# One more seven-product output pair for the sample, T sums made behind the merges, and new planner costs, in a hybrid encoder layer

## The chip, the core and the metric

The kernel runs on one core of a Trainium2 chip. The metric is the device time of one execution, in microseconds (us); the median of the runs shown is used. The engines are PE (TensorE: matmuls and transposes), DVE (VectorE), ACT (ScalarE), POOL (GpSimd) and SP (SyncE, which here issues every DMA). They run at the same time and wait for one another on semaphores.

## What is computed

One encoder layer is applied to two batches with the same weights: a prompt of 512 tokens and a sample of 1024 tokens, each token a row of 1024 numbers. Everything is float32.

```
h = rmsnorm(x)
proj = h @ w_in            # qa ka va za | qb kb vb zb | ga gb
oa = neighbourhood_attention(qa, ka, va, rpb_a) * silu(za)
oa = oa @ w_o_a
ob = window_gqa_attention(qb, kb, vb, t5_table, sink_b) * silu(zb)
ob = ob @ w_o_b
merged = sigmoid(ga) * oa + sigmoid(gb) * ob
y = x + merged @ w_out
```

`w_in` has 5376 columns, of which `ga` and `gb` are 1024 each; `w_out` is 1024 x 1024.

## The kernel before

**Products.** Each float32 operand is split in a rounded part and a remainder (`hi` and `lo`; `whi`, `wlo` for weights, `hh`, `hl` for activations). A product is hi·hi + hi·lo + lo·hi, three matmuls for each block of 128 rows. In the dense stages (`product`, L1284 to L1286) one product of a weight chunk with half of the rows takes 4 blocks x 3 matmuls of 128 x 512, summed in one bank of PSUM. ACT makes the rounded part and DVE or POOL the remainder (`split`, L1167 and L1172).

**Order of the stages.** Norm and attention of the prompt; dense stages of the prompt, with the norm of the sample beside them; attention of the sample; dense stages of the sample. A dense phase has pairs of z chunks (SiLU gates), pairs of gate chunks, eight merges and four output pairs. Some gate pairs are computed during attention already (`fill_gates`): for the sample the last two of eight.

**Plain and seven-product pairs.** A pair is two output chunks times two halves of the tokens. `pair_classic` makes it with eight products. `pair_strassen` makes it with seven, at the price of sums: four of weight tiles (`S`), and four of activations, `T`, which all pairs of a stage share. Its products 0, 1 and 6 read `hh` and `hl`, its products 2 to 5 read `T` 1, 2, 0 and 3. `CLASSIC_S` says how many pairs of z, gates and output are plain for the sample: 1, 0 and 2 before.

**T for the output stage.** `sums` builds each of the four `T` from merged activations, in four quarters k (`m` = k and k + 4), with ten additions a quarter of 128 x 512 (`tt`, L1161), into three `S` buffers. A quarter is then split into `T`. There are eight `T` buffers (four pairs of hi and lo). The gates' `T` hold them first, then the merges' operands `uv` (loaded back from DRAM: `ot<-u_d`, two buffers), then the output's `T`, in that turn. So each stage waits for the last reader of the stage ahead.

**The planner.** The order of all instructions is worked out when the program is built, by a list scheduler (`Flow.run`): an operation has engines that may take it, an estimated duration for each, and a priority (lower is sooner); when an engine is free in the planner's own clock, it takes the first ready operation by priority. A DMA costs SP 470 ns and lands after bytes / 360 ns behind the DMAs ahead. Buffers of the tags in `IN_TURN` are given out in program order. An operation that DVE or POOL may take counts as a port operation: the planner lets no port operation begin on one of the two while the other has one. On the chip each engine executes its list strictly in that order.

**The start.** The prompt's first tile is normed in four pieces: PE spreads the norm's gains over the partitions (L1629), DVE scales a piece (L520), PE transposes it (L532), ACT and DVE split it (L537, L542). Attention weights are loaded and split beside it (L600, L602, L607), the first remainder on POOL. Projections are L761.

Of the kernel before, what the change touches and what calls it, by code (L numbers as in the profile page):

```python
# [10 lines left out]
F32 = mybir.dt.float32  # L11
# [18 lines left out]
SIDE = {5: 0, 8: 1, 11: 2, 15: 3}  # L30
CLASSIC_S = (1, 0, 2)
LEFT_PAD = 56
WAKE = 0
SOON = 10
# [106 lines left out]
class Flow:  # L141
# [10 lines left out]

    IN_TURN = {"whi", "wlo", "w32", "T", "S", "raw", "U", "C", "ot"}

# [7 lines left out]
    def op(self, choice, emit, prio, new=(), use=(), into=(), after=(), hold=(), lag=0, port=None):  # L162

        o = Op()
        choice = tuple((e, ns * self.slack if e in ("act", "dve", "pool") else ns) for e, ns in choice)
        o.choice, o.emit, o.prio, o.new, o.lag = choice, emit, prio + self.base, list(new), lag
        o.key, o.outs, o.eng = len(self.ops), [], None
        o.port = {"dve", "pool"} <= {e for e, _ in choice} if port is None else port  # L170
        o.vals = {id(v): v for v in (*new, *use, *into, *hold)}.values()
        before = {id(a): a for v in use for a in v.writers}
        before.update({id(a): a for a in after if a is not None})
        for v in into:
            for a in v.writers[:1]:
# [12 lines left out]
    def dma(self, emit, nbytes, prio, **kw):  # L188
        return self.op((("sp", 470),), lambda e: emit(), prio, lag=nbytes / 360, **kw)

# [16 lines left out]
    def run(self):  # L207
# [59 lines left out]
        while done < len(self.ops):  # L267
            for e in ready:
                while free_at[e] <= now:
                    skipped, got = [], None  # L270
                    while ready[e]:
                        item = heapq.heappop(ready[e])
                        o = item[2]
                        if o.eng is not None:
                            continue
                        ns = dict(o.choice)[e]
                        if all(room(v, n) for v, n in o.new) and not any(locked(v, e) or v.held and not v.t for v in o.vals) and not barred(o, e) and all(
# [77 lines left out]
def encoder_kernel(  # L355
# [238 lines left out]
    def att_weights(src, n, prio, engs=("pool", "dve"), place=None, after=()):  # L594
# [11 lines left out]
        def emit(e):  # L606
            engines[e].tensor_tensor(lo.t[:, :n], sv(), hi.t[:, :n].bitcast(F32), op=ALU.subtract)  # L607

        f.op(
            tuple((e, {"pool": POOL_, "dve": DVE_}[e](n)) for e in engs), emit, prio, new=[lo], use=[hi], hold=[st], after=[a],  # L610
        )
# [36 lines left out]
    def attention_phase(geo, hh, hl, h_ops, mask_d, early, late):  # L648
# [24 lines left out]
        def tables(br, g, prio):  # L673
            nb_t = tile_([P, max(2 * at[-1], 4 * GW)], F32, "bias", 2)
            first = [nb_t]
            for i in range(2 if br == "A" else 4):
# [25 lines left out]
                else:  # L702
# [15 lines left out]

                    f.op((("act", ACT_(GW)),), emit, prio, new=first, use=[raw], into=[nb_t])
                    first = []  # L720
# [7 lines left out]
        def project(br, w, t, prio):  # L728
# [10 lines left out]
            else:  # L739
# [6 lines left out]
                for q in range(2):  # L746
                    for m, v in enumerate((hh, hl)):
                        done[m, q] = f.op(
                            (("act", 960), ("dve", DVE_(512))),
                            lambda e, m=m, v=v, q=q: copy(  # L750
# [96 lines left out]
        def make_qk(br, gi, t, qk, prio):  # L847
# [23 lines left out]
            elif whole:  # L871
# [13 lines left out]
            b = f.op(  # L885
                (("dve", DVE_(P) + 165),),
                lambda _: dve.scalar_tensor_tensor(
# [4 lines left out]
            for s in slots:  # L892
# [6 lines left out]
            f.op(  # L899
                (("dve", DVE_(n) + 165),),  # L900
                lambda _: dve.scalar_tensor_tensor(
# [234 lines left out]
    def dense_phase(geo, hh, hl, h_ops, o_stores, exps_done, start, opened, tp, up, p0, p1, p2, x_t, y_t, classic, fill, after_gates=None, side=None):  # L1136
# [8 lines left out]
        any_tt = lambda n: (("dve", DVE_(n)), ("pool", POOL_(n)))  # L1145
        u_d = dpool.tile([8, P, nt], F32, tag=f"u_d{nt}", name=f"u_d{nt}")
        g_d = dpool.tile([2, 8, P, nt], F32, tag=f"g_d{nt}", name=f"g_d{nt}")
        stores = {}
# [35 lines left out]

        def sums(prio, done):

            tv = [tuple(f.value(tp, [P, 4, sn], F32R, "T", 8) for _ in range(2)) for _ in range(4)]
            ops = {}
            for k in range(4):
                blk = lambda a, kk, n: (lambda: a.t[:, kk, n * sn : (n + 1) * sn].bitcast(F32))  # L1190
                h = {(i, n, a): blk((hh, hl)[a], k + 4 * i, n) for i in range(2) for n in range(2) for a in range(2)}
# [127 lines left out]

        def pair_strassen(srcs, post, prio, mov_h, mov_t, seed=None, last=False):  # L1320
            raw = {(m, i): load_raw(srcs[m][i], prio - 2) for m, i in ((0, 0), (1, 0), (1, 1), (0, 1))}
# [33 lines left out]
            )  # L1355
            result(0, 0, p1, mul(1, mov_h(1, 0)))
            add(u2, p1, mul(2, mov_t(1)))
# [158 lines left out]
        for i in range(8):  # L1516
# [9 lines left out]
            else:  # L1526
                pair_strassen(srcs, post, 4 + i, mov_h, mov_t)
            if side:
# [243 lines left out]
```

## Time and profile before

| What | us |
|---|---|
| Median of three runs | 1145.87 (1144.78 to 1147.69) |
| Profiled execution, device time | 1146.52 |
| Its span, first to last instruction | 1144.7 |
| PE busy | 1133.8 |
| DVE busy | 854.4 |
| ACT busy | 644.9 |
| POOL busy | 308.3 |
| Sample: gates end and merges begin | about 975 |
| Sample: merges end and output pairs begin | about 1060 |

Rows of a timeline give the start in us from the span's start, the duration, the engine, the line, the operation and its tiles (out<-in). A bracket at the end gives the idle time ahead of the operation and what ended it. Rows of waits give the total, the number and the longest. A row of groups by window gives the busy time of PE, PEld (weight loads), DVE, ACT and POOL with the number of instructions, then the granted clock, the DMA engines' share and GB/s.

### The profile page before, as it was taken

What the parts mean: (1) busy time and instruction counts of PE and PEld (TensorE: products, weight loads), DVE (VectorE), ACT (ScalarE), POOL (GpSimd) and SP (SyncE); (2) the same over time, 40 slices, a digit from 0 to 9 for tenths busy, and PEclk for the clock granted to TensorE, in tenths of its full rate; (3) what the DMA queues carried; (4) which work ended last, traced back from release to release, by engine and by line L of the source; (5) the groups of instructions that cost most, each with busy time, mean ns of one, the idle gap of its engine ahead of it and who ended that gap; (6) DMA issues with size and microseconds to landing.
All of it is one profiled execution on the core that took longest, in us unless ns stands there. A gap on an engine that the chain in (4) does not pass through costs nothing.

```text
span 1144.7 us, 18482 instructions
## 1 busy us (share of the span) xinstructions
PE 1133.8 (99%) x6139; PEld 985.8 (86%) x6139; DVE 854.4 (75%) x1975; ACT 644.9 (56%) x1467; POOL 308.3 (27%) x413
## 2 busy tenths in 40 slices
PE   8999999999999999999999999999999999999998
PEld 6999988888888899999999888888888888788887
DVE  5888798497765468887778888865878755497984
ACT  5777987544433346665678988865534434343320
POOL 3653433000010054343333445330222210132110
PEclk9999999999999999999999999999999999999999
DMA  7854543488786422121221213226657335573072
GB/s 253 273 158 141 181 113 102 115 264 266 232 277 199 165 72 67 25 70 32 71 61 50 56 37 93 56 66 214 218 148 211 129 111 159 200 238 121 29 223 90
DMA packets 124705, 159.86 MB, mean 140 GB/s; under 512 B 28297, under 2 KB 66961, under 8 KB 124610
## 3 DMA queue, kind: packets, MB, share of 16 engines
q1 hardware_dynamic: 124610, 158.69, 45.4%
q8 instruction: 48, 0.79, 0.3%
q14 instruction: 47, 0.39, 0.1%
HBM read 121.93 MB, written 41.44 MB: 143 GB/s over the span
## 4 chain that ended last, share of the span: by engine, by line
PE 94%; DVE 2%; DMA 2%; ACT 1%; POOL 1%; issue 0%; SPq 0%; ACTq 0%; POOLq 0%
PE p L761 25%; PE x L1285 9%; PE x L1286 9%; PE x L1284 9%; PE x L1063 5%; PE x L1026 5%; PE x L934 4%; PE p L1284 4%; PE p L1285 4%; PE d L1284 4%; PE p L1286 4%; PE d L1286 4%; PE d L1285 4%; PE x L861 2%; DMA ot<-u_d 1%; DMA w<-in_w_att_dram 1%
## 5 line engine op out<-in xcount | busy, mean ns | idle before, releaser
L761 PE MATMUL p<-whi,hh 128*128 128x384 f32 x384 | 133.4, 348 | 0.0
L761 PE MATMUL p<-wlo,hh 128*128 128x384 f32 x384 | 133.1, 347 | 0.0
L761 PE MATMUL p<-whi,hl 128*128 128x384 f32 x384 | 132.4, 345 | 0.0
L978 ACT ACTIVATE sb<-sb,mx 128x384 f32<-128x384 f32 (+1 forms) x192 | 107.5, 563 | 22.4 <-DVE mx L969 22.2
L1167 ACT ACTIVATE whi<-raw 128x512 fp32r<-128x512 f32 (+1 forms) x140 | 81.1, 590 | 52.6 <-PE x L1285 26.2
L761 PE MATMUL p<-whi,hb 128*128 128x384 f32 x384 | 107.5, 347 | 0.0
L1172 POOL TENSOR_TENSOR wlo<-raw,whi 128x512 fp32r<-128x512 f32 (+1 forms) x29 | 40.9, 1413 | 242.4 <-ACT whi L1167 130.4
L1284 PE MATMUL x<-hh,whi 128*128 128x512 f32 x264 | 102.7, 389 | 0.0
L1285 PE MATMUL x<-hl,whi 128*128 128x512 f32 x264 | 102.7, 389 | 0.0
L1286 PE MATMUL x<-hh,wlo 128*128 128x512 f32 x264 | 102.7, 389 | 0.0
L1037 DVE TENSOR_TENSOR pp<-x,pp 128x512 fp32r<-128x512 f32 (+1 forms) x136 | 82.6, 638 | 18.9 <-ACT pp L1032 17.8
L1172 DVE TENSOR_TENSOR wlo<-raw,whi 128x512 fp32r<-128x512 f32 (+1 forms) x111 | 70.1, 645 | 30.5 <-ACT whi L1167 30.2
L1285 PE MATMUL x<-T,whi 128*128 128x512 f32 x224 | 87.5, 390 | 0.3 <-DVE T L1172 0.2
L1286 PE MATMUL x<-T,wlo 128*128 128x512 f32 x224 | 87.2, 389 | 0.0
L1284 PE MATMUL x<-T,whi 128*128 128x512 f32 x224 | 87.1, 389 | 0.0
L1032 ACT ACTIVATE pp<-x 128x512 fp32r<-128x512 f32 (+1 forms) x136 | 70.9, 560 | 22.8 <-PE x L1026 21.8
L799 POOL TENSOR_TENSOR rs_r<-rs_v,mhalf 128x4 f32<-128x4 f32 (+1 forms) x72 | 81.7, 1134 | 5.7
L1063 PE MATMUL x<-pp,v 128*128 128x256 f32 (+1 forms) x368 | 77.8, 324 | 0.8 <-DVE pp L1037 0.8
L792 POOL TENSOR_SCALAR rs_v<-ss 128x4 f32<-128x4 f32 (+1 forms) x72 | 26.2, 364 | 187.3 <-DVE ss L785 184.6
L761 PEld LDWEIGHTS p<-whi,hl 128*128 128x128 f32 x384 | 73.0, 190 | 1.3 <-issue 1.0
L761 PEld LDWEIGHTS p<-wlo,hh 128*128 128x128 f32 x384 | 73.0, 190 | 1.0 <-issue 0.5
L761 PEld LDWEIGHTS p<-whi,hh 128*128 128x128 f32 x384 | 73.0, 190 | 0.9 <-issue 0.5
(351 smaller groups left out, 2985.5 us busy)
## 6 DMA issues: line engine op xcount, KB each, us to landing
raw<-in_w_g_dram SPq DMA_DIRECT2D x76, 256.0 KB
w<-in_w_att_dram SPq DMA_DIRECT2D x46, 384.0 KB
ot<-o_d SPq DMA_DIRECT2D x36, 256.0 KB
g_d<-C SPq DMA_DIRECT2D x34, 256.0 KB
raw<-in_w_z_dram SPq DMA_DIRECT2D x32, 256.0 KB
raw<-in_w_out_dram SPq DMA_DIRECT2D x32, 256.0 KB
C<-g_d SPq DMA_DIRECT2D x24, 256.0 KB
out_dram<-C SPq DMA_DIRECT2D x23, 256.0 KB
```

Source lines behind the costliest of these rows:

```text
L761: pe.matmul(ps.t[:, :GW], part[u](k), mv.t[:, c], start=k == 0 and m == 0, stop=k == KC - 1 and m == 2,)
L799: lambda e: nc.gpsimd.tensor_tensor(r.t[:, :nn], rv.t[:, :nn], mhalf[:, :nn], op=ALU.pow),
L978: act.activation(sb.t[:, :width], sb.t[:, :width], AF.Exp, bias=mx.t[:, i : i + 1], scale=-1.0, accum_out=sm.t[:, i : i + 1],)
L1026: pe.transpose(pt.t[:, u * P : (u + 1) * P], sbs[i].t[:, c * P : (c + 1) * P], ident)
L1032: lambda e, pt=pt, pp=pp, nn=nn: act.activation(pp.t[:, 0, :nn], pt.t[:, :nn], AF.Copy),
L1037: lambda e, pt=pt, pp=pp, nn=nn: dve.tensor_tensor(pp.t[:, 1, :nn], pt.t[:, :nn], pp.t[:, 0, :nn].bitcast(F32), op=ALU.subtract),
L1063: pe.matmul(out(), v.t[:, vs], mv(), start=first, stop=last)
L1167: (("act", ACT_(n)),), lambda e: act.activation(hi(), src(), AF.Copy), prio,
L1172: lambda e: engines[e].tensor_tensor(lo(), src(), hi().bitcast(F32), op=ALU.subtract), prio,
L1284: pe.matmul(out, hi.t[:, cs], mh(), start=first and k == 0, stop=False)
L1285: pe.matmul(out, hi.t[:, cs], ml(), start=False, stop=False)
L1286: pe.matmul(out, lo.t[:, cs], mh(), start=False, stop=last and k == len(ws) - 1)
```

## The change

- `CLASSIC_S` becomes (1, 0, 1): the sample's output pair 1 is a seven-product pair, so that of four output pairs one is plain.
- `sums` for the output stage gets priorities of its own, 19.2 to 19.5 for the quarters (the merges have 12 to 19, the output pairs 20 and more). The additions of the first three quarters no longer stay in `S` until a `T` is free: each of their twelve results is stored to DRAM (`to_d`), loaded into a `U` buffer at priority 20 and split into `T` from there, in the order of `T` 1, 2, 0, 3. The last quarter is split directly.
- In the sample's last seven-product gate pair (`free_t`) the second plain product comes behind the four products that read `T`.
- The planner counts DMAs with a priority below -2 at 230 bytes per ns, and matmuls before 13 us of its clock as 1.85 times as long. It counts the bias copy 76 ns longer, the `hb` copy on ACT 40 ns longer, and the scaled remainders of k and q on DVE 105 ns shorter. `hb` buffers are given out in program order, and each weight remainder of attention counts as a port operation. `SPREAD` is 0.

```
-CLASSIC_S = (1, 0, 2)
+CLASSIC_S = (1, 0, 1)
+SEED, SPREAD, SPAN, COLD = 0, 0, 1, 13000
+EARLY_RATE = 230
...
-    IN_TURN = {"whi", "wlo", "w32", "T", "S", "raw", "U", "C", "ot"}
+    IN_TURN = {"whi", "wlo", "w32", "T", "S", "raw", "U", "C", "ot", "hb"}
...
+        if self.slack != 1:
+            o.prio += SPREAD * (hash((SEED, o.key // SPAN)) % 1000 / 1000 - 0.5)
...
-        return self.op((("sp", 470),), lambda e: emit(), prio, lag=nbytes / 360, **kw)
+        return self.op((("sp", 470),), lambda e: emit(), prio, lag=nbytes / (EARLY_RATE if prio < -2 else 360), **kw)
...
-                        ns = dict(o.choice)[e]
+                        ns = dict(o.choice)[e] * (1.85 if e == "pe" and now < COLD and o.prio > -20.5 else 1)
...
-            ... new=[lo], use=[hi], hold=[st], after=[a],
+            ... new=[lo], use=[hi], hold=[st], after=[a], port=True,
...
-                    f.op((("act", ACT_(GW)),), emit, prio, new=first, use=[raw], into=[nb_t])
+                    f.op((("act", ACT_(GW) + 76),), emit, prio, new=first, use=[raw], into=[nb_t])
...
-                            (("act", 960), ("dve", DVE_(512))),
+                            (("act", 1000), ("dve", DVE_(512))),
...
-                (("dve", DVE_(P) + 165),),
+                (("dve", DVE_(P) + 60),),
...
-                (("dve", DVE_(n) + 165),),
+                (("dve", DVE_(n) + 60),),
...
+        to_d = dpool.tile([4, 4, P, sn], F32, tag=f"to_d{nt}", name=f"to_d{nt}")
...
-        def sums(prio, done):
+        def sums(split_prio, done, prios=None):
...
+                prio = prios[k] if prios else split_prio
...
                 for j in (0, 2, 1, 3):
-                    vh, vl = tv[j]
-                    ops[j, k] = split(
-                        lambda vh=vh, k=k: vh.t[:, k], lambda vl=vl, k=k: vl.t[:, k], lambda v=t[j]: v.t[:, :sn], sn, prio,
-                        (vh, k == 0), (vl, k == 0), [t[j]],
+                    if prios and k < 3:
+                        away.append((j, k, dma(
+                            lambda j=j, k=k, v=t[j]: nc.sync.dma_start(to_d[j, k], v.t[:, :sn]), 512 * sn, prio, use=[t[j]]
+                        )))
+                    else:
+                        away.append((j, k, t[j]))
+            for j, k, v in sorted(away, key=lambda a: ((1, 2, 0, 3).index(a[0]), a[1])) if prios else away:
+                vh, vl = tv[j]
+                if prios and k < 3:
+                    o, v = v, tile_("U", 4)
+                    dma(
+                        lambda j=j, k=k, v=v: nc.sync.dma_start(v.t[:, :sn], to_d[j, k]), 512 * sn, split_prio, new=[v],
+                        after=[o],
                     )
+                ops[j, k] = split(
+                    lambda vh=vh, k=k: vh.t[:, k], lambda vl=vl, k=k: vl.t[:, k], lambda v=v: v.t[:, :sn], sn, split_prio,
+                    (vh, j not in firsts), (vl, j not in firsts), [v],
+                )
+                firsts[j] = True
...
-        def pair_strassen(srcs, post, prio, mov_h, mov_t, seed=None, last=False):
+        def pair_strassen(srcs, post, prio, mov_h, mov_t, seed=None, last=False, free_t=False):
...
-            result(0, 0, p1, mul(1, mov_h(1, 0)))
+            if not free_t:
+                result(0, 0, p1, mul(1, mov_h(1, 0)))
             add(u2, p1, mul(2, mov_t(1)))
             add(u3, u2, mul(3, mov_t(2)))
             b = mul(4, mov_t(0))
             add(u4, u2, b)
             result(1, 1, u3, b)
             result(1, 0, u3, mul(5, mov_t(3)), ALU.subtract)
+            if free_t:
+                result(0, 0, p1, mul(1, mov_h(1, 0)))
...
-                pair_strassen(srcs, post, 4 + i, mov_h, mov_t)
+                pair_strassen(srcs, post, 4 + i, mov_h, mov_t, free_t=i + 1 == 8 - fill)
...
-        mov_h, mov_t = blocks(m_ops, nh), sums(20, m_ops) if o_classic < 4 else None
+        mov_h, mov_t = blocks(m_ops, nh), sums(20, m_ops, [19.2 + 0.1 * k for k in range(4)]) if o_classic < 4 else None
```

More of the change, by code (lines that the diff above doesn't have):

```diff
@@ L609, in att_weights @@
         f.op(
-            tuple((e, {"pool": POOL_, "dve": DVE_}[e](n)) for e in engs), emit, prio, new=[lo], use=[hi], hold=[st], after=[a],
+            tuple((e, {"pool": POOL_, "dve": DVE_}[e](n)) for e in engs), emit, prio, new=[lo], use=[hi], hold=[st], after=[a], port=True,
         )
@@ L1183, in moving_sums @@
             return mov
-        def sums(prio, done):
+        def sums(split_prio, done, prios=None):
             tv = [tuple(f.value(tp, [P, 4, sn], F32R, "T", 8) for _ in range(2)) for _ in range(4)]
-            ops = {}
+            ops, away, firsts = {}, [], {}
             for k in range(4):
+                prio = prios[k] if prios else split_prio
                 blk = lambda a, kk, n: (lambda: a.t[:, kk, n * sn : (n + 1) * sn].bitcast(F32))
```

## Prediction

> **What bounds the kernel now.** I read the page first: the share of each engine, then the chain that ended last.
>
> ```profile
> span 1144.7 us, 18482 instructions
> PE 1133.8 (99%) x6139; PEld 985.8 (86%) x6139; DVE 854.4 (75%) x1975; ACT 644.9 (56%) x1467; POOL 308.3 (27%) x413
> PE 94%; DVE 2%; DMA 2%; ACT 1%; POOL 1%; issue 0%; SPq 0%; ACTq 0%; POOLq 0%
> ```
>
> TensorE (PE) is busy 1133.8 of 1144.7 us and is 94% of the chain. So a change pays in two ways only: fewer matmuls, or a shorter wait of PE. The view of PE's waits has all of the second kind:
>
> ```profile
> PE x L1629 <- DMA rb<-in_norm_row_dram: 4.4, 1, 4.4
> PE x L861 <- DVE qk L816: 1.0, 2, 0.5
> PE x L532 <- DVE xt L520: 0.9, 1, 0.9
> PE x L1063 <- DVE pp L1037: 0.8, 2, 0.6
> PE x L1026 <- DVE sb L1010: 0.3, 1, 0.3
> PE x L1285 <- DVE T L1172: 0.2, 1, 0.2
> ```
>
> Columns: total us, times, longest. The first is the load that opens the kernel, and no edit makes it shorter. The rest sums to 3.2 us. The profiled execution took 1146.52 us, 1.8 more than its span and 0.65 above the median of 1145.87; the sum below is made against it, and the prediction is the median less the same gain.
>
> A busy PE is not a paced PE, since the records of neighbouring matmuls overlap. The pace is read from starts. These are the first matmul of the sample's output stage and the first that reads a T there, in PE's timeline (start, duration):
>
> ```profile
> 1059.71 0.39 PE L1284 MATMUL x<-hh,whi 128*128 128x512 f32 x1
> ...
> 1108.67 0.39 PE L1284 MATMUL x<-T,whi 128*128 128x512 f32 x1
> ```
>
> Between them lie two plain pairs and two products of the third pair. A plain pair is 8 products of 4 x 3 matmuls, 96; so 2 x 96 + 2 x 12 = 216 matmuls in 48.96 us, **226.7 ns each**, not the 389 ns that the records last.
>
> **Term 1, one output pair with seven products.** With one plain pair instead of two, pair 1 has 7 x 12 = 84 matmuls for 96. 12 x 226.7 ns = **2.7 us** of PE work gone, on the chain. Its weights cost four more additions and three more splits on VectorE (DVE) and POOL; they are counted in term 4.
>
> **Term 2, the moved plain product of the gates.** In the last seven-product gate pair the second plain product runs after the four that read T. Each T is read for the last time one product, 12 x 226.7 ns = 2.7 us, earlier, and the merges' operands are loaded into the same buffers. What PE loses there now, and what it waits for:
>
> ```profile
> 975.15 0.40 PE L1284 MATMUL x<-T,whi 128*128 128x512 f32 x1
> 975.76 0.50 PE L1285 MATMUL x<-T,whi 128*128 128x512 f32 x1 [0.22 <-DVE T L1172]
> ...
> 979.06 0.39 PE L1284 MATMUL x<-T,whi 128*128 128x512 f32 x1
> 979.57 0.50 PE L1285 MATMUL x<-T,whi 128*128 128x512 f32 x1
> ```
>
> ```profile
> 967.11 4.66 DMA ot<-u_d
> ...
> 973.18 4.96 DMA ot<-u_d
> ```
>
> Starts 0.61 and 0.51 us apart instead of 0.23: 0.38 + 0.28 = 0.7 us lost, less than the 2.7 us by which the buffers come free. The second view (the chain, in order of time) says that loads of 4.66 and 4.96 us, two in flight, paced the T. They may start earlier with the buffers, so I take **0.7 us**, with 0 as the other end if something else paces them. The moved product's result, sigmoid and store come later too, and so does p1's U buffer; the merges' first use of U is over 20 us behind, which covers it.
>
> **Term 3, the start.** DVE's remainder of the second weight with scalings 3 and 4 of the first tile behind it, then PE's gain rows and first projections (start, duration):
>
> ```profile
> 8.72 0.96 DVE L607 TENSOR_TENSOR wlo<-w,whi 128x768 fp32r<-128x768 f32 x1 [1.17 <-ACT whi L602]
> 9.60 0.86 DVE L520 SCALAR_TENSOR_TENSOR xt<-xt,nr,x 128x256 f32<-128x256 f32 x2
> ```
>
> ```profile
> 4.42 3.75 PE L1629 MATMUL x<-rb,one 1*128 1x256 f32 x8 [4.42 <-DMA rb<-in_norm_row_dram]
> ...
> 10.92 0.67 PE L761 MATMUL p<-whi,hh 128*128 128x384 f32 x1
> ...
> 12.03 0.52 PE L761 MATMUL p<-whi,hh 128*128 128x384 f32 x1
> 12.35 0.52 PE L761 MATMUL p<-wlo,hh 128*128 128x384 f32 x1
> ...
> 16.98 0.33 PE L761 MATMUL p<-whi,hh 128*128 128x384 f32 x1
> 17.15 0.33 PE L761 MATMUL p<-wlo,hh 128*128 128x384 f32 x1
> ```
>
> Before, the planner believes the second weight to be early and puts its remainder ahead of scalings 3 and 4. At 230 bytes per ns it is planned later, and POOL's remainder of the first weight (now a port operation) bars it meanwhile, so the scalings should go first. They need the gain rows, done at 4.42 + 3.75 = 8.17; an estimate of 8.5 replaces 9.60, and the first projection comes some 0.9 us sooner than 10.92. But matmuls are 0.32 us apart there (12.03 to 12.35) and 0.17 later (16.98 to 17.15), though the clock column shows full speed: 0.9 us of slow time holds 2.8 matmuls, worth 0.5 us once fast. Some of that is lost again at the qk wait (1.0 in two waits), so I take **0.4 us**; ends: 0.9 lost, if another order starves PE, and 0.9 won, if the fast pace begins sooner as well. The Trainium skill (TensorE: Matmul & The Clock Gate, Part 1) ties the fast pace to free-running activity windows of 3.4 us; by that the 0.5 before the loss would stand, and 0.9 could not be counted on.
>
> The other planner costs (scalings of k and q, hb, the bias copy, hb in turn) change no instruction, only its order. I take 0. In attention PE waits 1.0 + 0.8 + 0.3 = 2.1 us in all, which is the most a better order wins; a worse one may lose as much. SPREAD is 0 and moves nothing.
>
> **Term 4, sums behind the merges: its cover.** The sums of the first three quarters are made while merges run, stored (12 DMAs of 256 KB), loaded again (12 more) and split. PE now needs a T at 1059.71 + (96 + 24) x 0.2267 = **1086.9**, not 1108.7. What the vector engines had free (columns: window, then busy us of PE, PEld, DVE, ACT, POOL), and how long the sums last on DVE:
>
> ```profile
> 1032.00:1064.00 32.00, 32.00 (x142) 26.49 (x142) 25.72 (x37) 11.23 (x19) 8.85 (x6) 1.00 0.37 119
> 1062.00:1090.00 28.00, 28.00 (x125) 23.20 (x124) 28.00 (x47) 9.80 (x16) 1.42 (x2) 1.00 0.05 14
> ```
>
> ```profile
> 1073.13 2.49 DVE L1161 TENSOR_TENSOR S<-S,hl 128x512 f32<-128x512 f32 x4
> ...
> 1088.17 2.48 DVE L1161 TENSOR_TENSOR C<-x,C 128x512 f32<-128x512 f32 x4
> ```
>
> DVE is full to 1090 and ends the sums at 1088.17: left alone they would be late. But it is idle 6.3 of the 32 us before 1064. One operation takes (2.49 - 0.69)/3 = 0.60 us. From 1032 to 1086.9 (54.9 us) there are 28 operations of other work before 1064 (the 37 of the first window less 9 on S and T, 16.8), 40 sums (24.0), 16 remainders of T (9.6) and some 4 us of results and pair 1's weights: about 54.4, all on DVE. POOL takes some: it was busy 8.85 us in the first window. So it fits, **0 us**, with little left. The last quarter can't start before the last merge is split, which I put some 5 us behind 1059.71, at 1065, and needs 10 x 0.60 = 6 us, then its splits: done near 1082 for the last T, which is read three products after the first. The DMAs have room: their share is 0.37 and 0.05 in the two windows. Two trips of 4.96 us cost some 10 us, covered for the quarters that were ready by 1064. If the cover is gone, PE waits in pair 1; the first two rivals price it.
>
> **Sum:** 2.7 + 0.7 + 0.4 = 3.8 us; 1146.5 - 3.8 = 1142.7 for the profiled execution, **1142.1** for the median. 0.3% of the median, about what a measurement can tell from no change, is 3.4 us: the forecast lies only just beyond.
>
> **Rivals.**
> *DVE becomes the bound at pair 1 (0.25).* For it: 54.4 of 54.9 us. Pair 1's first weights are planned behind sums and T, yet PE wants them 24 matmuls earlier, at 1081.5. POOL's help has a price:
>
> ```profile
> 1001.41 4.71 POOL L1172 TENSOR_TENSOR wlo<-raw,whi 128x512 fp32r<-128x512 f32 x3
> ...
> 1003.20 1.78 DVE L1172 TENSOR_TENSOR hl<-C,hh 128x512 fp32r<-128x512 f32 x1
> ```
>
> Beside POOL a DVE operation lasted 1.78 us, not 0.69: 1.1 lost. Two such meetings, less the 0.5 that DVE has left, make PE wait 2 x 1.1 - 0.5 = 1.7 us: 1143.8. It decides from the moment when DVE's work up to 1086.9 passes 54.9 us. Against it: the planner keeps port operations apart. The Trainium skill (SBUF — State Buffer, "SBUF: two separate sides") calls the port pair of DVE and GpSimd an exclusive lock that a two-input DVE operation also meets, the loser standing for the whole instruction; the 1.78 us agree.
>
> *The DRAM trip is late, the slower side (0.08).* SP issues in order, and it stood once for 23.7 us behind one DVE result:
>
> ```profile
> SPq L1457 <- DVE C L1161: 24.1, 3, 23.7
> ```
>
> If a store stands like that until 1088 ahead of the loads, three rounds in four U buffers follow, 3 x 4.96 = 14.9 us: T at about 1103, PE 16 us late, 1158. It decides from 7.2 us on (3.8 given back, 3.4 lost), a T later than 1094. Against it: the first three quarters are ready well before, and the loads follow in the plan's own order.
>
> *The new order loses in attention or at the start (0.12).* The 2.1 us of waits there double: 1144.2.
>
> *The moved product frees nothing (0.07).* The loads, not the buffers, pace the T; the 0.7 stays: 1142.8.
>
> **How the numbers follow.** The forecast has 0.48; its own range is 1140.4 (1.7 more from start and attention) to 1143 (the start's gain and half of term 2 missing). The range 1140.4 to 1145.6 takes in all but the DRAM trip, the far tail of the DVE rival and a doubly good order. Faster by over 0.3% (below 1142.4): most of the forecast and a lucky share of the attention case, 0.47. Within 0.3%: the rest of the forecast, the other rivals, 0.44. Slower by over 0.3% (above 1149.3): the DRAM trip and a bad tail, 0.09.
>
> **What would show it.** PE with 6127 matmuls. Term 2: no start more than 0.25 us apart in the first T products of the merges. Term 3: both pairs of scalings ahead of the second remainder, first projection near 10. Term 4: PE's starts unbroken over pair 1, DVE with S work in the merges, no wait of PE for T or wlo behind them; SP without a wait over 10 us while T loads. It is wrong if PE waits over 1 us in the output stage, or if attention's waits move by more than 2 us.

## The result, and the profile after

The changed kernel takes 1159.68 us (median of 4 runs, 1158.69 to 1161.3); the kernel before took 1146.78 beside it. The ratio is **1.0114, interval 1.0085 to 1.0142**: about 13 us slower, where 3.8 us faster was forecast. The profiled execution of after took 1159.02 us.

The page of after, in the lines that answer to those of before:

```profile
span 1156.5 us, 18522 instructions
PE 1134.1 (98%) x6127; PEld 983.1 (85%) x6127; DVE 871.0 (75%) x1980; ACT 641.1 (55%) x1474; POOL 323.2 (28%) x423
PE 83%; DVE 6%; DMA 5%; ACT 2%; POOL 2%; issue 2%; SPq 1%; DVEq 0%; POOLq 0%; ACTq 0%
```

PE has the 12 matmuls fewer, yet 0.3 us more of busy time, since those at a lower clock lasted longer. The chain tells more: PE was 94% of it and is 83%. Eleven per cent have gone to engines and transfers that PE waits for. The view of PE's waits (total us, times, longest) names them:

```profile
PE p L1305 <- ACT whi L1172: 5.4, 1, 5.4
PE x L1654 <- DMA rb<-in_norm_row_dram: 4.7, 1, 4.7
PE p L765 <- DVE hb L668: 2.1, 1, 2.1
PE x L865 <- DVE qk L820: 1.6, 3, 0.7
PE p L1307 <- DVE wlo L1177: 1.5, 1, 1.5
PE x L1305 <- ACT T L1172: 1.4, 1, 1.4
```

(Lines have moved by a few: `product` is L1305 to L1307 now, projections are L765, `split` is L1172 and L1177, sums are L1166.) The second row is the load that opens the kernel, as before. All others are new or larger. The first and the fifth are in the output stage, the third and fourth in the prompt's attention, the sixth where the merges begin.

To place the loss I added up PE's starts in the trace: for each matmul the time to the next start, less the median of that time for its shape over the traces of this study (0.227 us for 128x512). The rest, the **excess**, is what PE lost, summed by stretch (us; the last stretch of after begins with its output pairs at 1064.62):

| Stretch of the span | before | after |
|---|---|---|
| 0 to 20 (start) | 4.7 | 3.1 |
| 20 to 140 (attention of the prompt) | 5.1 | 10.5 |
| 140 to 400 (the prompt's rest) | 3.5 | 3.9 |
| 400 to 960 (sample: attention, gates) | 16.3 | 15.6 |
| 960 to 1000 (gates end, merges begin) | 1.0 | 2.1 |
| 1000 to 1060 (merges) | -0.1 | -0.1 |
| 1060 to the end (output pairs) | -0.1 | 9.5 |
| all | 30.4 | 44.7 |

(Rows add up to within 0.1 by rounding.) So 14.3 us were lost and 2.7 us of matmuls saved: 11.6 of the 11.8 us by which the span grew. **Two places carry it**, attention (5.4) and output pair 1 (9.6).

PE's timeline at the first products of pair 1 that read T (start, duration, then what ended the idle time), and the window from there (PE, PEld, DVE, ACT, POOL, granted clock, DMA share, GB/s):

```profile
1091.79 0.40 PE L1307 MATMUL p<-hh,wlo 128*128 128x512 f32 x1
1097.54 0.79 PE L1305 MATMUL p<-T,whi 128*128 128x512 f32 x1 [5.35 <-ACT whi L1172]
1098.13 0.63 PE L1306 MATMUL p<-T,whi 128*128 128x512 f32 x1
1100.27 0.80 PE L1307 MATMUL p<-T,wlo 128*128 128x512 f32 x1 [1.51 <-DVE wlo L1177]
1100.86 0.63 PE L1305 MATMUL p<-T,whi 128*128 128x512 f32 x1
1101.28 0.63 PE L1306 MATMUL p<-T,whi 128*128 128x512 f32 x1
```

```profile
1097.00:1104.00 7.00, 4.95 (x12) 3.50 (x13) 6.29 (x12) 3.40 (x7) 0.57 (x1) 0.54 0.58 173
```

Three losses stand here. PE started nothing from 1091.79 to 1097.54, 5.75 us for 0.23: 5.5 lost. Two matmuls later it stood again, 1098.13 to 1100.27: 1.9 lost. And the matmuls behind are 0.42 us apart (1100.86 to 1101.28) at a granted clock of 0.54: the other 2.1 of the 9.5.

The releaser of the first wait is a weight, `whi`, not T. ACT's timeline says why it was late:

```profile
1094.62 0.63 ACT L1172 ACTIVATE T<-U 128x512 fp32r<-128x512 f32 x1 [2.87 <-DMA U<-to_d]
...
1095.85 0.63 ACT L1172 ACTIVATE T<-U 128x512 fp32r<-128x512 f32 x1
...
1096.87 0.62 ACT L1172 ACTIVATE whi<-S 128x512 fp32r<-128x512 f32 x1
```

The two sums that this weight is made of, on DVE and POOL, stand in the timeline too:

```profile
1093.19 0.69 DVE L1166 TENSOR_TENSOR S<-raw 128x512 f32<-128x512 f32 x1
1093.95 1.27 POOL L1166 TENSOR_TENSOR S<-S,raw 128x512 f32<-128x512 f32 x1 [7.78 <-DMA C<-in_xt_s_dram]
```

The chain, in order of time, says what was behind that:

```profile
1079.85 4.25 DMA out_dram<-C
...
1084.12 0.33 SPq L1468
...
1084.56 3.98 DMA U<-to_d
...
1090.87 4.96 DMA U<-to_d
...
1095.85 0.64 ACT T L1172
...
1096.51 1.29 DVE T L1177 x2
1097.81 0.60 DVE C L1166
...
1099.61 0.61 DVE wlo L1177
1100.27 0.80 PE p L1307
```

ACT works its list in order. It stood 2.87 us for a reload of a T quarter, did the splits of T that its list has first, and only then the weight that PE wanted. That order is some 1.6 us of the wait, since the weight's second sum ended only at 1095.22 (1093.95 + 1.27) and its split lasts 0.62; the rest lies with the sums, which stood behind T's remainders on DVE (`w_first` below comes back to them). On DVE the other weight's remainder stands behind two T remainders and more in the same way. The reloads come in rounds of four U buffers, each some 4 to 5 us long, and one of them stood on SP behind a load of `C` (L1468) that waited for a store of `out_dram`.

### The profile page after: what moved, and what is told of

It reads as the page before. It is cut to its first block, busy times and chain, and to the rows that moved or that the text cites. A ratio compares the mean times of both kernels' runs of the same rounds, so it can differ in the third digit from the quotient of the medians.

```text
span 1156.5 us, 18522 instructions
## 1 busy us (share of the span) xinstructions
PE 1134.1 (98%) x6127; PEld 983.1 (85%) x6127; DVE 871.0 (75%) x1980; ACT 641.1 (55%) x1474; POOL 323.2 (28%) x423
## 4 chain that ended last, share of the span: by engine, by line
PE 83%; DVE 6%; DMA 5%; ACT 2%; POOL 2%; issue 2%; SPq 1%; DVEq 0%; POOLq 0%; ACTq 0%
PE p L765 21%; PE x L1306 8%; PE x L1307 8%; PE x L1305 8%; PE x L1067 5%; PE x L1030 4%; PE x L938 4%; PE p L1307 4%; PE p L1305 4%; PE p L1306 4%; PE d L1305 4%; PE d L1307 3%; PE d L1306 3%; PE x L865 1%; DVE S L1166 1%
## 5 line engine op out<-in xcount | busy, mean ns | idle before, releaser
L765 PE MATMUL p<-whi,hh 128*128 128x384 f32 x384 | 132.9, 347 | 0.0
L765 PE MATMUL p<-whi,hl 128*128 128x384 f32 x384 | 132.3, 345 | 0.0
L765 PE MATMUL p<-wlo,hh 128*128 128x384 f32 x384 | 131.1, 342 | 0.2 <-DVE wlo L611 0.2
L982 ACT ACTIVATE sb<-sb,mx 128x384 f32<-128x384 f32 (+1 forms) x192 | 107.7, 564 | 29.7 <-DVE mx L973 29.3
L765 PE MATMUL p<-whi,hb 128*128 128x384 f32 x384 | 109.1, 347 | 2.1 <-DVE hb L668 2.1
L1172 ACT ACTIVATE whi<-raw 128x512 fp32r<-128x512 f32 (+1 forms) x140 | 79.9, 586 | 49.1 <-PE x L1306 24.1
L1306 PE MATMUL x<-hl,whi 128*128 128x512 f32 (+1 forms) x264 | 102.0, 386 | 0.0
L1305 PE MATMUL x<-hh,whi 128*128 128x512 f32 (+1 forms) x264 | 102.0, 386 | 0.0
L1307 PE MATMUL x<-hh,wlo 128*128 128x512 f32 (+1 forms) x264 | 101.9, 386 | 0.0
L1177 DVE TENSOR_TENSOR wlo<-raw,whi 128x512 fp32r<-128x512 f32 (+1 forms) x106 | 70.4, 670 | 33.6 <-ACT whi L1172 33.5
L1305 PE MATMUL x<-T,whi 128*128 128x512 f32 x232 | 90.4, 390 | 1.4 <-ACT T L1172 1.4
L1306 PE MATMUL x<-T,whi 128*128 128x512 f32 x232 | 90.4, 389 | 0.2 <-DVE T L1177 0.2
L1307 PE MATMUL x<-T,wlo 128*128 128x512 f32 x232 | 90.2, 389 | 0.0
L1177 POOL TENSOR_TENSOR wlo<-raw,whi 128x512 fp32r<-128x512 f32 (+1 forms) x34 | 49.1, 1453 | 142.3 <-ACT whi L1172 112.2
L803 POOL TENSOR_TENSOR rs_r<-rs_v,mhalf 128x4 f32<-128x4 f32 (+1 forms) x72 | 84.7, 1176 | 5.8
L765 PEld LDWEIGHTS p<-whi,hb 128*128 128x128 f32 x384 | 69.7, 189 | 5.8 <-DVE hb L668 2.4
L765 PEld LDWEIGHTS p<-wlo,hh 128*128 128x128 f32 x384 | 72.5, 189 | 1.5 <-issue 0.7
L765 PEld LDWEIGHTS p<-whi,hl 128*128 128x128 f32 x384 | 72.4, 188 | 1.7 <-issue 1.3
```

What stands on the lines that cost most here:

```text
L765: pe.matmul(ps.t[:, :GW], part[u](k), mv.t[:, c], start=k == 0 and m == 0, stop=k == KC - 1 and m == 2,)
L803: lambda e: nc.gpsimd.tensor_tensor(r.t[:, :nn], rv.t[:, :nn], mhalf[:, :nn], op=ALU.pow),
L982: act.activation(sb.t[:, :width], sb.t[:, :width], AF.Exp, bias=mx.t[:, i : i + 1], scale=-1.0, accum_out=sm.t[:, i : i + 1],)
L1172: (("act", ACT_(n)),), lambda e: act.activation(hi(), src(), AF.Copy), prio,
L1177: lambda e: engines[e].tensor_tensor(lo(), src(), hi().bitcast(F32), op=ALU.subtract), prio,
L1305: pe.matmul(out, hi.t[:, cs], mh(), start=first and k == 0, stop=False)
```

## Experiments: which part loses

Each run is compared with the kernel before on the same chip; "before" in a diff is the kernel before, and lines that a diff doesn't show are as it says in words. No run leaves out or changes any part of the computation.

**Planner costs alone** (`planner_only`): after, with two plain output pairs, old sums and the product of the gates in its old place.

```
-CLASSIC_S = (1, 0, 1)
+CLASSIC_S = (1, 0, 2)
-... free_t=i + 1 == 8 - fill)
+... free_t=False)
-... sums(20, m_ops, [19.2 + 0.1 * k for k in range(4)]) ...
+... sums(20, m_ops) ...
```

> Only the planner costs of the change (230 bytes per ns for the first loads, slow matmuls before 13 us, hb in turn, the port flag, the corrected ACT and DVE durations) on the kernel before; two plain output pairs, old sums, old order of the gates. Theory A (the new order loses in attention by itself): 4 to 5 us longer than before, with PE's first sample projection 4 to 5 us later (before 395.1) and a wait of PE for an hb copy near 120 us. Rival B (the costs are neutral, and what the trace of after shows in attention follows from the other parts): within 1 us of before.

Measured: 1150.31 us, ratio 1.0037 (1.0024 to 1.0050): 4.0 us longer, the outcome of theory A. Its wait for `hb` is 0.5 us, though, where after has 2.1.

**Output pair and moved product alone** (`output_only`), with all planner costs of before (rates, 13000 to 0, `hb` out of `IN_TURN`, no `port`, old durations).

```
-SEED, SPREAD, SPAN, COLD = 0, 0, 1, 13000
-EARLY_RATE = 230
+SEED, SPREAD, SPAN, COLD = 0, 0, 1, 0
+EARLY_RATE = 360
```

> Only the output part (one plain pair, sums behind the merges, moved gate product) with the planner's old costs. Theory A (two separate losses; pair 1 waits behind reloaded sums whatever came before): PE waits 7 to 9 us at the first T products of pair 1 and the time is 5 to 8 us above before. Rival B (pair 1 waits only because the new costs shift the plan): no wait over 1 us there, 3 us below before.

Measured: 1154.61 us, 1.0074 (1.0057 to 1.0091), 8.3 us above before where 5 to 8 were expected. The excess is 10.4 us in the output stage and 5.4 in the prompt's attention, where before has 5.1. PE's waits at pair 1's first T products are 3.1 and 2.0 us, less than the 7 to 9 expected; 1.8 of the 10.4 stand in pair 0, where PE waits 1.6 us for a remainder of merged activations. The two parts add up: 0.37% and 0.74% are 1.11%, against 1.14% for the whole change.

**The moved product of the gates alone** (`free_only`: `free_t` as in after, all else as before).

> Only the moved plain product in the last seven-product gate pair. The prediction's term 2: the 0.7 us at the first T products of the merges go, PE's starts there stay 0.23 us apart. Rival (the loads pace the T, and their order or landing decides): 0.5 to 2 us remain or are added there, as the 1.55 and 0.28 us in the trace of after. Time within 1.5 us of before in either case.

Measured: 1146.93 us, 1.0005 (0.9994 to 1.0015): nothing. The chain of this run where the merges begin:

```profile
970.70 1.31 POOL T L1177
...
972.03 5.01 DMA ot<-u_d
...
977.06 0.64 ACT T L1172
...
978.47 0.50 PE x L1306
```

T buffers were free sooner, and it made no difference: the operand of the merges has only two `ot` buffers, and one was held until 972.01 by a remainder that the planner now gives to POOL (1.31 us for DVE's 0.70). The load behind it took 5.01 us. The last such load of before started at 973.18.

**Seven-product pair with the old sums** (`classic_old_sums`: the output part of after, no trip through DRAM, no moved product).

```
-... sums(20, m_ops, [19.2 + 0.1 * k for k in range(4)]) ...
+... sums(20, m_ops) ...
```

> Only one plain output pair instead of two, with the sums as before (not ahead of their T buffers, no DRAM). Sums ended at 1088 on DVE before, and T is wanted at about 1087: PE should wait 2 to 8 us before pair 1's first T product and the time be 0 to 5 us above before. Rival (the 21.8 us of the dropped pair were never needed as cover): no wait, 2.7 us below before.

Measured: 1153.13 us, 1.0069 (1.0044 to 1.0094), 6.8 us above before where 0 to 5 were expected. One wait carries it:

```profile
PE p L1307 <- DVE wlo L1177: 7.1, 1, 7.1
```

It is in pair 1's second product, ahead of any that reads T: the weight's remainder stands on DVE behind all the sums. So the trip through DRAM, made to avoid this, cost about what it saved.

## Experiments: is it DVE's work or its order

The windows of after and of a run of those below, `late_ot`, over the 57.2 us up to the moment at which pair 1 wants its first T (96 + 24 matmuls, 27.2 us, behind the begin of the output pairs), answer the question of capacity:

```profile
1034.60:1091.80 57.20, 57.20 (x254) 47.06 (x252) 53.22 (x71) 18.11 (x32) 23.78 (x15) 1.00 0.61 193
```

```profile
1030.80:1088.00 57.20, 57.20 (x253) 47.06 (x253) 54.71 (x75) 18.14 (x32) 26.19 (x16) 1.00 0.63 198
```

`late_ot` (the second) has DVE busy 54.7 us and POOL 26.2, more than after, and its first T product starts on time, 27.4 us behind the begin of its output pairs (1060.78 to 1088.21). By then 12 of T's 16 remainders are done; the other four follow beside the T products. So the same work can be done with PE waiting little, and what differs is which work comes first. These runs took it apart, all with the planner costs of before and the output part of after.

**Weights first** (`w_first`): sums and splits of pair 1's weights at priority 19.8 for 20.5, ahead of T's splits (20).

```
-            w = weight_tiles([raw[0, 0], ...], 6, prio - 0.5)
+            w = weight_tiles([raw[0, 0], ...], 6, w_prio)
...
+                ... w_prio=19.8 if i == o_classic else None)
```

> The output part alone (old planner costs), with pair 1's weight sums and splits at priority 19.8, ahead of the splits of the reloaded T (20); nothing else differs from the run output_only, which took 1154.61 and waited 3.2 + 2.2 us for whi and wlo at the first T product. Theory A (T is there in time; the weights only stand behind T's splits in the lists of ACT and DVE, which wait for the reload): the waits for whi and wlo go, no more than 1.5 us for T takes their place, 4 to 7 us below output_only. Rival B (the reloaded T itself is late): PE waits as long as before, for T; within 1.5 us of output_only.

Measured: 1152.0 us, 1.0051 (1.0034 to 1.0068): 2.6 us below `output_only`, between the two outcomes written down. The wait for `wlo` went from pair 1's first T products, that for `whi` grew from 3.1:

```profile
PE p L1305 <- ACT whi L1172: 4.6, 1, 4.6
```

The code has a reason: `S` has three buffers, given out in program order, so the sums s1 and s2 of pair 1's weights take buffers that sums of the last quarter hold until T's splits have read them, and those splits come behind reloads. Whatever their priority, by the code the weights hang on the reloads by way of a buffer.

**Reloads counted later** (`tod_late`): the planner counts each load of `to_d` 2.2 us later. Its own figure for 256 KB, from issue to landing with no transfer ahead, is 470 + 650 + 728 (bytes / 360) + 950 ns, 2.8 us; the chain above has 3.98 and 4.96.

```
-                        at(dma_free + 950, 2, got)
+                        at(dma_free + 950 + got.late, 2, got)
...
-                        after=[o],
+                        after=[o], late=LATE,
```

> The output part alone, with the planner told that a load from to_d lands 2.2 us later than by its own formula (the trace has 4.7 to 5.0 us from issue to landing, the formula gives about 2.8). Theory A' (the loss comes from a plan that believes the reloads early, so that engines stand in fixed order behind them): the waits of PE at pair 1 fall from 5.8 us to under 2, 4 to 6 us below output_only. Rival B (capacity of DVE or of the loads, whatever the order): within 1.5 us of output_only.

Measured: 1150.46 us, 1.0026 (1.0006 to 1.0046). That is 4.2 us below `output_only`, as the theory had it. PE's waits in pair 1 are 2.6 and 0.4 us, more than the 2 expected, and the excess in the output stage is 3.5 us for 10.4, in an execution of 1147.53 us, 2.9 below this run's median. With lists made for a later landing, less stands behind a reload.

**Weight sums out of the S ring** (`ot_sums`): s1 and s2 of the output pairs go to the two `ot` buffers, which are free by then; reloads counted as in the change.

```
-            s1, s2, s3, s4 = (tile_("S", 3, 512) for _ in range(4))
+            s1, s2, s3, s4 = (tile_(*(("ot", n_ot) if seed and k < 2 else ("S", 3)), 512) for k in range(4))
```

> As late_ot, but the planner counts the loads of to_d as the change does. It tells the two halves of the order apart. If the S ring alone held pair 1's weights: no PE wait over 1 us, as late_ot, ratio 0.997 to 0.999. If the early planning of the splits of T counts as well: pair 1's first T product waits 1.5 to 4 us for T, not for whi or wlo, ratio 1.000 to 1.004. If DVE's work is the cause: waits for wlo as in the output part alone, ratio 1.005 to 1.008.

Measured: 1158.93 us, 1.0104 (1.0091 to 1.0117), worse than any. PE's timeline and DVE's there:

```profile
1082.69 0.39 PE L1306 MATMUL d<-hl,whi 128*128 128x512 f32 x1
1094.41 0.80 PE L1307 MATMUL d<-hh,wlo 128*128 128x512 f32 x1 [11.33 <-DVE wlo L1177]
```

```profile
1088.90 0.68 DVE L1166 TENSOR_TENSOR S<-S,hl 128x512 f32<-128x512 f32 x1
1090.60 0.69 DVE L1177 TENSOR_TENSOR T<-U,T 128x512 fp32r<-128x512 f32 x1 [1.02 <-ACT T L1172]
1091.21 0.68 DVE L1166 TENSOR_TENSOR C<-x,C 128x512 f32<-128x512 f32 x1
...
1093.67 1.36 DVE L1177 TENSOR_TENSOR wlo<-raw,whi 128x512 fp32r<-128x512 f32 x3
```

Now even a plain weight of pair 1, which needs no sum and no T, stands behind remainders of T on DVE, and those behind reloads: DVE was idle 1.02 us ahead of one of them while PE waited 11.3 us; for 9.1 of these it worked, on pieces that its list has first. Neither outcome with a small wait that I had written down came true; the early count of the reloads does harm even where these sums don't use the ring.

**Both** (`late_ot`): reloads counted later and the weight sums in `ot`.

> The output part and the moved gate product, with the planner's costs of before; the planner counts the loads of to_d 2.2 us later than it did, and the two weight sums s1 and s2 of each output pair are made in the two free ot buffers instead of the S ring. Theory that the wait of 3 to 5 us before the first T products came from a fixed order (weight sums tied by the three S buffers to the splits of T, and splits planned before the loads land): no PE wait over 1 us between the output pairs' begin and end, 84 matmuls in place of 96, so 2.7 us less than before less some 0.5 us: ratio 0.997 to 0.999, some 1144 us. Rival that DVE has too much work there, whatever the order: PE still waits 3 us or more for whi, wlo or T in pair 1, ratio 1.001 to 1.005.

Measured: 1145.96 us, 0.9996 (0.9986 to 1.0005). The loss of the output part is gone, but the 0.997 to 0.999 expected was not reached. The two longest of PE's waits behind the opening load:

```profile
PE x L1306 <- ACT T L1173: 1.3, 1, 1.3
PE x L1308 <- DVE wlo L1178: 1.0, 1, 1.0
```

The first is where the merges begin, the second in pair 1. The 2.7 us are used up by these: excess 1.4 in the output stage (before none) and 2.1 at the begin of the merges (before 1.0).

Since any edit changes the order, this could be a lucky one. Eight traces speak against that. The four runs that have the sums behind the merges and the early count (after, `output_only`, `w_first`, `ot_sums`) have an excess of 8.4 to 16.0 us in the output stage; the four with the later count (`tod_late`, `late_ot` and the two that follow) have 1.4 to 3.5. The ring shows only beside the later count: `tod_late` took 1.0026 with it, `late_ot` 0.9996 without.

**Without the moved product** (`late_ot_nofree`: `free_t=False`), asked since the move had shown no gain:

> late_ot without the moved gate product. In the traces with the moved product one of the four remainders behind it goes to POOL (1.3 us for 0.7), the buffer that it frees is loaded last, and the load that paces the merges' first T comes no sooner. Theory that the move costs: the starts at the first T products of the merges lose 0.7 us as in the kernel before, not 2.0; 1.3 us less than late_ot, ratio 0.9980 to 0.9990. Rival that it frees buffers and so gains, as the prediction's second term says: 0.5 us or more slower than late_ot, ratio 1.0000 to 1.0010. Rival that it counts for nothing: 0.9996.

Measured: 1145.22 us, **0.9983 (0.9972 to 0.9994)**, 12 runs, 1.4 us below before's 1146.6. It is the only run whose whole interval lies below 1, by little, and one of sixteen: some of it may be luck. The trace of this run, of an execution of 1148.42 us, its slowest, doesn't show the reason that I expected: its excess at the begin of the merges is 2.6 us, and that of `late_ot` 2.1. The two ratios overlap, so that the move costs anything isn't shown.

**And with the weights of pair 1 first** (`late_ot_nofree_w`: the edit of `w_first` on top):

> late_ot_nofree with the weight sums and weight splits of output pair 1 at a priority ahead of the splits of T (19.8 for 20.5; T has 20). Theory that the last 1.1 us there are the remainder of s2 standing behind two splits of T: no start over 0.3 us apart in pair 1, 1.1 us less than late_ot_nofree, ratio 0.997 to 0.998. Rival that the T then comes late instead: a PE wait for T of 1 us or more at pair 1's first T product, ratio as late_ot_nofree or above, 0.998 to 1.001.

Measured: 1145.96 us, 0.9996 (0.9983 to 1.0010), not the 0.997 to 0.998 of the theory. The wait for `wlo` went, and T came late in its place, though in a later product than the first that reads it (1098.20, the first is at 1088.68):

```profile
PE x L1307 <- DVE T L1178: 2.8, 3, 2.4
```

## Experiments: what loses in attention

The new planner costs change no operation, only the order and, where an operation may run on two engines, which of them takes it. Which of these costs loses? Each run below is the kernel before with one of them, or with a change of the same kind that the change doesn't have.

**Remainders of k and q 105 ns shorter, alone** (`stt_only`: `DVE_(P) + 165` and `DVE_(n) + 165` become `+ 60`):

> The kernel before with one change: the planner counts the scaled remainders of k and q on DVE 105 ns shorter (before 1.1 slack). Theory C (this is what loosens the attention order: the reserve that covered results landing later than planned is gone): 2 to 5 us above before, PE's first sample projection at 397 to 400 instead of 394 to 395. Rival D (it is the start's costs or the hb, port and bias costs): within 1 us of before.

**The start's rate and slow matmuls, alone** (`start_only`: `EARLY_RATE = 230`, `COLD = 13000`):

> The kernel before with two changes of the planner: first loads at 230 bytes per ns and matmuls 1.85 times as long before 13 us. Theory D (the loss of attention starts here: the first order fits, but the loads of bias tables and next weights behind it come later): 2 to 5 us above before, first projection near 10.0, PE waits for qk of 1 us or more near 29 and 53 us, first sample projection 397 to 400. Rival C (the shorter k and q durations are the cause): first projection near 10.0 and 0 to 1 us below before.

**All the other new costs** (`hb_port_bias`: `hb` in turn, `port=True`, `+ 76`, 1000 for 960):

> The kernel before with the rest of the new planner costs alone: hb in turn, weight remainders as port operations, bias copy 76 ns and hb copy 40 ns longer. If only the shorter remainders and the start's costs lose: ratio 0.999 to 1.001. If the order is what matters, a loss here too is likely: 1.002 to 1.005.

**Remainders only 5 ns shorter** (`stt_160`: `+ 165` becomes `+ 160`):

> The kernel before, where the planner counts the scaled remainders of k and q 5 ns shorter (the change has 105 ns). If the loss of stt_only (0.48%) comes from the size of the cost, a twentieth of it loses nothing that can be measured: ratio 0.999 to 1.001. If any change of order can lose: up to 1.004, with the excess of PE's starts spread over several places of the prompt's attention and the dense stage behind it.

**Exponential 4 ns longer** (`exp_186`: `ACT_(width) + 182` becomes `+ 186`):

> The kernel before, where the planner alone counts one exponential of attention 4 ns longer (186 for 182 ns on top of its size): the instructions are the same, their order in attention another. Theory that attention's order in the kernel before happens to fit the chip and nearly any other loses: PE's waits in attention rise by 2 us or more, 1148.5 to 1151 us, ratio 1.002 to 1.0045. Rival that the loss of the new planner costs comes from their sizes (durations counted shorter leave less room): a longer count loses nothing, ratio 0.9985 to 1.001.

**The factor on all durations** (`slack_111`: `SLACK = 1.1` becomes 1.11):

> The kernel before, where the planner's factor on durations is 1.11 instead of 1.1: all counted durations with the factor 0.9% longer, so a little more room, and another order. Theory of the fitting order: ratio 1.002 to 1.0045, with waits of PE in attention that stand at other places than in the runs of the new costs. Rival of the sizes: ratio 0.9985 to 1.001.

Measured, with the excess of the profiled execution by stretch (us):

| Run | us | ratio (interval) | 0 to 20 | 20 to 140 | 140 to 400 |
|---|---|---|---|---|---|
| before | 1146.3 to 1146.6 | | 4.7 | 5.1 | 3.5 |
| all planner costs | 1150.31 | 1.0037 (1.0024 to 1.0050) | 3.0 | 9.6 | 6.0 |
| k and q shorter | 1151.11 | 1.0048 (1.0029 to 1.0066) | 2.5 | 11.8 | 5.3 |
| start | 1151.28 | 1.0049 (1.0028 to 1.0070) | 3.2 | 9.7 | 5.4 |
| the others | 1152.02 | 1.0045 (1.0031 to 1.0059) | 3.5 | 8.3 | 4.6 |
| k and q 5 ns shorter | 1154.25 | 1.0062 (1.0049 to 1.0076) | 3.5 | 14.3 | 3.6 |
| exponential 4 ns longer | 1150.77 | 1.0035 (1.0023 to 1.0048) | 2.5 | 6.6 | 8.1 |
| factor 1.11 | 1145.45 | 0.9992 (0.9981 to 1.0003) | 2.8 | 6.6 | 5.2 |

Five nanoseconds cost no less than 105, a longer count loses like a shorter one, and three disjoint groups of costs lose as much singly as together. So the sizes of the costs don't carry the loss. **The order does**, with the choice of engines that belongs to it: any of these edits shuffles the whole list of attention. Before's order of PE's work there is in ten traces (before and all runs with its costs), with an excess from 20 to 400 of 8.6 to 11.0 us. The seven new orders have 11.8 to 17.9. Six lost 0.35 to 0.62%; one, the factor 1.11, came out even, which is what the rival of the sizes had written down for it (its trace is of an execution of 1148.29 us, 2.8 above its median). The number of instructions that POOL takes doesn't tell them apart: before has 413, the worst 428, the even one 425. Waits of PE in the worst of them:

```profile
PE x L861 <- DVE qk L816: 3.8, 4, 2.9
PE x L1026 <- DVE sb L1010: 3.1, 4, 1.2
```

How a list that looks equally good loses is seen in the chain of after, at its longest wait in attention:

```profile
116.36 5.91 DMA w<-in_w_att_dram
...
122.29 0.85 ACT whi L606
...
123.39 0.44 ACT sb L982 x2
...
125.06 0.51 DVE hb L668
```

A weight's load took 5.91 us, and its split had been put at a fixed place of ACT's list. The exponentials (L982) stood behind it, though their data was there, `hb` behind them, and PE 2.1 us behind `hb`. The order of before has no such meeting of that length. A part of it is that execution's: `planner_only` has PE's same order in attention, there the load took 4.31 us, and PE's wait for `hb` was 0.5. Why before has none, and whether an order could be chosen for that without the chip, stays open.

## Why the prediction was wrong

- **"12 x 226.7 ns = 2.7 us of PE work gone"**: right. 6127 matmuls, and the work at the median pace is 2.7 us less.
- **"So it fits, 0 us, with little left"** (term 4): the step that failed most, worth 9.6 us in after. That the work can be done was right, in `late_ot`, but not as counted (54.4 of 54.9 us, all on DVE): DVE's 75 operations there took 54.7 us, 0.73 each for the 0.60 counted, POOL did 16 more in 26.2, and four of T's 16 remainders came later. Above all, capacity is no cover. The step left out that each engine works a list in fixed order, that the list was made with reloads of 2.8 us where 4 to 5 passed, and that `S`, by the code, ties the weights to T's splits. "Two trips of 4.96 us cost some 10 us, covered for the quarters that were ready by 1064" was wrong as well: the twelve reloads go through four U buffers, which came free one by one, and the last was issued at 1090.87.
- **The rivals.** "DVE becomes the bound at pair 1" had the place, and `classic_old_sums` shows its mechanism where the trip is left out (7.1 us). For after, the nearest was the one that got 0.08, "the DRAM trip is late", with its reloads in rounds, a load that stood in SP's order, and a T product later than 1094 as its mark: 1097.54. It put the wait in one long stand of SP; it was the order of ACT and DVE, and the sums behind it. That its price, 1158, is near the 1159.68 measured is luck: 9.6 us of the loss stand in the output stage, and 5.4 in attention, for 16 in the output stage alone.
- **"The other planner costs … I take 0", at most 2.1 us either way**: failed. The costs alone lost 4.0 us (`planner_only`), 5.4 us of excess in attention in after. PE's waits of before bound what a better order can win; they say nothing of what a worse one can lose. The rival for it doubled the same 2.1, and so was too small as well.
- **"They may start earlier with the buffers, so I take 0.7 us"** (term 2): failed. `free_only` lost nothing and won nothing. The rival "The loads, not the buffers, pace the T" was right, with POOL's remainder in the chain besides. "The merges' first use of U is over 20 us behind" was misread: the first sum into U is at 999.4, but its loads take U buffers from 966.58 on. No loss from that shows.
- **"First projection … some 0.9 us sooner than 10.92"** (term 3): it came at 9.96, behind both pairs of scalings, as forecast. But 10.92 was a late draw: with the costs of before, ten profiled executions have it from 10.17 to 10.92 (median 10.35), and three with the new costs of the start from 9.60 to 9.96 (median 9.83). So the first projection comes some 0.5 us sooner by the order. What of it reaches the end can't be seen, since the same costs lose more in attention.
- The range ended at 1145.6 since it left out the DRAM trip and bounded what a new order can lose by waits of before. The two terms that failed most are of one kind: a new order priced at nothing.

## What to carry to other kernels

Where engines follow lists made ahead, a free engine is no cover: follow what stands ahead of the needed instruction on its engine, up to the load that this waits for, and count that load as the trace has it. An edit that changes no instruction but reorders a stretch is an unknown of its own (here from no difference to 0.6% worse), and the waits of before bound only its gain. Look also for small rings of buffers that tie two streams of work together: in `w_first` a priority alone took away only 2.6 of 8.3 us.

## What was not expected of the hardware

**A wait of a few us can cost PE its pace for some us more.** After 5.35 us of idle time the matmuls of after were 0.43 us apart for 0.23, at a granted clock of 0.54, and the pace was back at 1103.4. In `ot_sums`, after 11.3 us, 0.43 held until 1100.5. In two runs a gap of about 2 us was followed by it too, later: with the exponential 4 ns longer, 2.32 us passed from one start to the next, PE soon ran at 0.23 again, and then

```profile
359.46 0.39 PE L1284 MATMUL x<-hh,whi 128*128 128x512 f32 x1
359.69 0.39 PE L1285 MATMUL x<-hl,whi 128*128 128x512 f32 x1
...
360.30 0.63 PE L1284 MATMUL x<-hh,whi 128*128 128x512 f32 x1
360.72 0.63 PE L1285 MATMUL x<-hl,whi 128*128 128x512 f32 x1
...
363.28 0.44 PE L1285 MATMUL x<-hl,whi 128*128 128x512 f32 x1
363.56 0.39 PE L1286 MATMUL x<-hh,wlo 128*128 128x512 f32 x1
```

slowed to 0.42 us from start to start, until 363.28, some 3.4 us at a granted clock of 0.51, with no wait at all. The other such run is `w_first`, after 1.86 us from start to start. Gaps of 2.75 and 2.96 us, counted in the same way, in `late_ot_nofree_w` and `tod_late` were followed by nothing of the kind. The Trainium skill (TensorE: Matmul & The Clock Gate, Part 1) tells of free-running activity windows of 3.4 us and has the slow state come after at least one idle window. The length here, 3.4 us, agrees with that; the gaps of 2.32 and 1.86 us, shorter than a window, don't, and the measurement decides. What makes one gap of 2 to 3 us cost the pace and another not stays open.
